# W_down of a decoder layer by seven block products, with tokens as the stationary operand

## The chip, the cores and the metric

One core of a Trainium2 chip runs the whole kernel as one program. The metric is the device time of one execution in microseconds; three runs of the kernel before gave 1706.38, 1706.41 and 1708.55 us, median 1706.41. A profiled execution gives the trace that is read here. Its span runs from the first to the last instruction.

TensorE multiplies: a stationary operand of up to 128 x 128 is loaded into its array, and a moving operand of up to 512 columns streams through it into PSUM. VectorE (DVE), ScalarE (ACT) and GpSimd (POOL) do elementwise work; SyncE (SP) issues most transfers. Each engine has its own queue and works through it in order.

## The reference

One layer, 288 tokens (256 of a prompt, 8 x 4 samples), width 2048. The part that matters here is the feed-forward half:

```python
x = layer_norm(ALPHA * x + merged @ w_o, ln1_g, ln1_b)
hid = jnp.square(jax.nn.relu(x @ w_up))              # 2048 -> 8192
x = layer_norm(ALPHA * x + hid @ w_down, ln2_g, ln2_b)   # 8192 -> 2048
```

Before it stand the input projection, a short convolution, a gated delta rule with its states, two output projections, a gated merge and `w_o`. They are the same in both kernels. All inputs and outputs are float32.

## The kernel before, in words

**Three matmuls for one.** A float32 product is made of fp32r matmuls. Each weight block of 512 KB (4 x 128 rows by 256 columns, `raw`) is split: ScalarE casts it to `hi` (`split_hi`, line 179), VectorE subtracts, `lo = raw - hi` (`split_lo`, line 140 in the helper `tt`). The activations have their own high and low parts. The weights stand in the array, 128 x 128 at a time, and the 288 tokens stream: high by high, high by low, low by high (lines 206 to 208).

**Order.** `blocks` is one long list of weight blocks. The main loop takes block `i`: it splits block `i+3`, runs what is due at `i` (evacuations, side work), issues the 24 matmuls of block `i`, and loads block `i+7`. `raw`, `hi` and `lo` have four buffers each. The load on SP's queue waits until VectorE has read the old `raw`.

**Feed-forward.** The 8192 hidden features are taken in four stages of 2048. In a stage, `w_up` makes 8 groups of 256 features (`up_evac`, line 501: norm of the input, ReLU, square, high and low parts `hh`, `hl`), then `w_down` makes 8 groups of 256 output features, summed feature-major in `acc` by VectorE (`down_evac`, line 528). The residual was written there before, during the first up stage (`residual1`, line 477).

**End.** In the last W_down stage each finished group is transposed to token-major (`turned`, line 601) and its statistics are taken. The last two groups are 128 features wide. `final` (line 642) joins the statistics, makes the last norm with small matmuls of rank 3, which carry mean and scale per row, and sends out. Its constants are loaded by `tail_consts` (line 561) and `tail_tiles` (line 575); `tail_rows` (line 592) splits the rows of gain and bias.

Of the kernel before, what the change touches and what calls it, by code (L numbers as in the profile page):

```python
# [16 lines left out]
P = 128  # L17
# [5 lines left out]
KT = D // P  # L23
H = 8
# [16 lines left out]
def _constants():  # L41
# [33 lines left out]
    f["rowlo"] = np.isin(k, (1, 4)) * 1.0  # L75
    early = ("hm", "bo8", "lcum", "lrem", "lcums", "lrems", "lsp", "bm3", "hmask")
    late = ("quart", "rowhi", "rowlo")
# [26 lines left out]
def hybrid_kernel(ctx: ExitStack, tc: tile.TileContext, A):  # L104
# [9 lines left out]
    ap_ = pool("ap")  # L114
    acp = pool("acp", 2, space=PSUM)
# [43 lines left out]
    fill = []  # L159

    def at(i, f):
        due.setdefault(i, []).append(f)


    def load(i):
        if i >= len(blocks):
            return
        gi, r0, k0, _, _ = blocks[i]
        t = wp.tile([P, KB, GW], F32, tag="raw", name=nm("raw"))
# [3 lines left out]
        raw[i] = t  # L173

    def split_hi(i, step=KB):
        if i < len(blocks):
            his[i] = wp.tile([P, KB, GW], F32R, tag="hi", name=nm("hi"))
            for k in range(0, KB, step):
                act.copy(his[i][:, k:k + step], raw[i][:, k:k + step])  # L179

    def split_lo(i, step=KB):
        if i < len(blocks):
            los[i] = wp.tile([P, KB, GW], F32R, tag="lo", name=nm("lo"))
            r = raw.pop(i)
            for k in range(0, KB, step):
                tt(los[i][:, k:k + step], r[:, k:k + step], his[i][:, k:k + step], SUB)

    def matmuls(i):
        gi, r0, k0, first, last = blocks[i]
        if first:  # L190
            gi["ps"] = acp.tile([P, 2, 512], F32, tag="acc", name=nm("acc"))
# [26 lines left out]
    ci = cp.tile([P, CI.shape[1]], I32, name="ci")  # L218
# [19 lines left out]
    hw = cp.tile([P, 24, 28], F32, name="hw")  # L238
    hwa = cp.tile([P, 8, 19], F32, name="hwa")
    lnp = cp.tile([P, 33], F32, name="lnp")  # L240
    wbar = ao0[:, NL - NE:NL - NE + 16 * KT].rearrange("p (k c) -> p k c", c=16)
    arow = cp.tile([P, 2, 8], F32, name="arow")
    epsc = cp.tile([P, 3], F32, name="epsc")
    hmr, bo8 = (cp.tile([P, P], F32R, name=n) for n in ("hmr", "bo8"))
    stB = cp.tile([P, 24, 27], F32, name="stB")
    stA = cp.tile([P, 8, 18], F32, name="stA")
# [130 lines left out]
    def yb_evac(p):  # L377
        def f(ps):
# [4 lines left out]
            t = ph["pool"].tile([P, 2, NT], F32, tag="yt", name=nm("yt"), bufs=2)  # L383
# [13 lines left out]
    def wo_evac(p):  # L397
        q = slice(2 * p, 2 * p + 2)

        def resid(ps):  # L400
            pl = ph["pool"]
            if p == 0:
# [4 lines left out]
                ph["ln"] = [t[:, 5 + u] for u in range(4)]  # L407
# [4 lines left out]
            ph["s"] = pl.tile([P, 2, NT], F32, tag="yt", name=nm("s"), bufs=2)  # L412
# [49 lines left out]
    def norms(ps):  # L462
# [4 lines left out]
        dm, va, av, nb = ph["ln"]  # L467
# [7 lines left out]
        ph["acc"] = ph["pool"].tile([P, KT, NT], F32, tag="R1", name="acc")  # L475

    def residual1(p):
        tl = {}

        def f():  # L480
            _, _, av, nb = ph["ln"]
            q = slice(2 * p, 2 * p + 2)
            t = ph["pool"].tile([P, 2, NT], F32, tag="yt", name=nm("x1"), bufs=2)
# [7 lines left out]
        def f2():  # L491
            for u in range(2):
                k = 2 * p + u
                act.activation(ph["acc"][:, k, :], tl["t"][:, u, :], AF.Identity, bias=lnp[:, 16 + k:17 + k],
                               scale=ALPHA)
        return f, f2
# [4 lines left out]
    def up_evac(c, p):  # L501
        tl = {}

        def f(ps):
            pl = ph["pool"]
            _, _, av, nb = ph["ln"]
            if p == 0:
                ph["hh"] = xp.tile([P, KT, NT], F32R, tag="XH", name=nm("hh"))
                ph["hl"] = xp.tile([P, KT, NT], F32R, tag="XL", name=nm("hl"))
            s = slice(2 * p, 2 * p + 2)  # L510
            r = pl.tile([P, 2, NT], F32, tag="sg", name=nm("r"), bufs=2)
            q = pl.tile([P, 2, NT], F32, tag="yt", name=nm("r2"), bufs=2)
            w = pl.tile([P, 2, 2], F32, tag="w2", name=nm("w2"), bufs=2)
            act.copy(w, ps[:, :, NT:NX])
            tt(q, ps[:, :, 0:NT], bmid(av, 2), MUL)
            for u in range(2):
                stt(q[:, u, :], nb, w[:, u, 0:1], q[:, u, :], MUL, ADD)
                act.activation(r[:, u, :], q[:, u, :], AF.Relu, bias=w[:, u, 1:2])
            tt(q, r, r, MUL)
            tl["q"] = q  # L520

        def f2(ps):
            s = slice(2 * p, 2 * p + 2)
            act.copy(ph["hh"][:, s, :], tl["q"])
            tt(ph["hl"][:, s, :], tl["q"], ph["hh"][:, s, :], SUB)
        return [f, f2]

    def down_evac(c, p):
        def f(ps):
            a = ph["acc"][:, 2 * p:2 * p + 2, :]  # L530
            tt(a, a, ps[:, :, 0:NT], ADD)
        if c == 3:
            if p == 0:
                return [f, lambda ps: None, lambda ps: out_tiles(p)]
            hold = []

            def rest(ps):
                for g in hold:
                    for _ in g:
                        pass  # L540
                if p < 5:
                    tail_rows(p - 1)
            return [f, lambda ps: None, lambda ps: hold.extend(filter(None, [out_tiles(p)])), rest]
        return [f]

    def next_to_last(ps):
        a = ph["acc"][:, 14, :]
        tt(a, a, ps[:, 0, 0:NT], ADD)

    def collect(ps):  # L550
        turned(14)
        fin, bn = ph["fin"], ph["bn"]
        for b in range(2):
            dve.bn_aggr(out=fin[:, b, 1:3], in_=bn[:, b, 0:15])
        dve.tensor_scalar(out=fin[:, :, 2], in0=fin[:, :, 2], scalar1=15.0 * P, scalar2=None, op0=MUL)

        R = ph["R"] = ph["pool"].tile([P, 2, 2, 6], F32R, tag="mv", name="R")
        act.copy(R[:, 1, :, 3:5], bc(ones[:, 0:2], 2))
        act.mul(R[:, 1, :, 5], ones[:, 0:2], 0.0)

    def tail_consts():
        g3 = ph["pool"].tile([P, KT, NT], F32, tag="R2", name="g3").rearrange("p k t -> p (k t)")
        ph["g2"] = g3[:, 0:D]
        ph["gs"], ph["bs"], ph["b0"] = (g3[:, D + 512 * u:D + 512 * u + 512] for u in range(3))
        ph["late"] = g3[:, D + 1536:D + 1536 + CF.shape[1] - NL]
        gps.dma_start(ph["g2"][:, 1024:D], A["ln2_g"][:, 1024:D].to_broadcast([P, D - 1024]))
        gps.dma_start(ph["b0"], A["ln2_b"][:, 1024:1536].to_broadcast([P, 512]))
        gps.dma_start(ph["late"], A["cf"][:, NL:])
        for j in range(4):
            for t, n in (("gs", "ln2_g"), ("bs", "ln2_b")):  # L570
                row = A[n].rearrange("o (k j f) -> o k j f", j=4, f=P)[:, :, j, :]
                gps.dma_start(ph[t][32 * j:32 * j + 32, :].rearrange("p (k f) -> p k f", k=4),
                              row.to_broadcast([32, 4, P]))

    def tail_tiles():
        pl = ph["pool"]
        g4 = pl.tile([P, D + 512], F32R, tag="R4", name="g4")
        ph["m5"], ph["st5"] = g4[0:6, 0:D], g4[0:6, D:D + 512]
        r5 = pl.tile([P, KT * NX], F32, tag="R3", name="r5")
        ph["r5"] = r5[:, 0:2 * D].rearrange("p (a c) -> p a c", a=2)  # L580
# [874 lines left out]
```

## Time and profile before

| what | value |
|---|---|
| median of three runs | 1706.41 us |
| span of the profiled execution | 1703.4 us |
| TensorE busy | 1688.5 us, 99% of the span |
| VectorE, ScalarE, GpSimd busy | 1007.2, 734.1, 133.8 us |
| `lo` on VectorE, 128 x 1024 | 492 times, mean 1239 ns |
| `hi` on ScalarE, 128 x 1024 | 492 times, mean 1046 ns |
| W_down matmuls | 3 x 1024, 288 columns each, from 968.5 to 1687.9 us in four stages |
| mean granted TensorE clock | 0.998 |

How to read the rows: a matmul's duration overlaps its neighbours', so the spacing of starts is its price, not its mean. In a row of a group stand line, engine, operation, output and inputs, shapes and count, then total busy time and mean of one in ns, then the engine's idle time ahead of them with what ended it. In a timeline row stand start, duration, engine, line and operation; "x2" joins two neighbours. In a row of stages stand the window, its length, and busy time with the number of instructions for PE, PEld (weight load), DVE, ACT and POOL, then the granted clock, the transfers' share and GB/s. In the chain of waits the second number of a row is the time that the piece held the end.

### The profile page before, as it was taken

Reading aid. Unit: us, or ns where it says so; the run is one execution under the profiler, and the core shown is the slowest. Engines: PE = TensorE matmul, PEld = TensorE weight load, DVE = VectorE, ACT = ScalarE, POOL = GpSimd, SP = SyncE. Lnnn points to the kernel's source line nnn. Section 1 sums busy time; section 2 is a strip of 40 time slices with the busy share of each in tenths; the row PEclk is TensorE's granted clock in tenths of the full one; section 3 lists DMA queues with packets and bytes.
Section 4 is the critical chain, followed back from the end, with each engine's and each line's share of the span. In section 5 each row is a group of like instructions: output and inputs, shape, how many; then the busy total and the mean of one; then the engine's idle time right before and its main releaser. Section 6 shows DMA issues by size and latency. Waiting matters only on the chain.

```text
span 1703.4 us, 31106 instructions
## 1 busy us (share of the span) xinstructions
PE 1688.5 (99%) x13063; PEld 1668.7 (98%) x13063; DVE 1007.2 (59%) x1296; ACT 734.1 (43%) x1067; POOL 133.8 (8%) x223
## 2 busy tenths in 40 slices
PE   9999999999999999999999999999999999999997
PEld 7999999999999999999999999999999999999997
DVE  5577876758544444456778844566445654466565
ACT  4675626333543333334445533444334433344442
POOL 2232412023300000000010000000000000000000
PEclk9999999999999999999999999999999999999999
DMA  8464456435555555555565555555555555555552
GB/s 244 140 194 139 123 175 200 150 115 180 162 170 169 166 162 170 163 164 165 158 190 174 165 170 161 164 170 162 167 168 161 163 171 162 164 167 164 162 162 80
DMA packets 275097, 279.18 MB, mean 164 GB/s; under 512 B 13131, under 2 KB 270092, under 8 KB 274952
## 3 DMA queue, kind: packets, MB, share of 16 engines
q1 hardware_dynamic: 270414, 265.95, 51.3%
q0 software_dynamic: 4256, 11.12, 2.3%
q8 instruction: 102, 1.67, 0.4%
q14 instruction: 37, 0.30, 0.1%
q10 hardware_dynamic: 288, 0.13, 0.0%
HBM read 269.68 MB, written 7.48 MB: 163 GB/s over the span
## 4 chain that ended last, share of the span: by engine, by line
PE 98%; DVE 1%; DMA 0%; POOL 0%; issue 0%; SPq 0%; ACT 0%; POOLq 0%; ACTq 0%
PE acc L206 31%; PE acc L208 31%; PE acc L207 31%; PE g L1084 1%; DMA xr<-in_x_prompt_dram 0%; PE g L1072 0%; PE g L1231 0%; PE g L1251 0%; PE g L831 0%; DVE w L143 0%; PE g L1254 0%; PE g L1203 0%; PE g L1243 0%; PE g L608 0%; PE g L798 0%; PE g L958 0%
## 5 line engine op out<-in xcount | busy, mean ns | idle before, releaser
L140 DVE TENSOR_TENSOR lo<-raw,hi 128x1024 fp32r<-128x1024 f32 (+2 forms) x502 | 614.0, 1226 | 556.2 <-ACT hi L179 553.7
L179 ACT CAST hi<-raw 128x1024 fp32r<-128x1024 f32 (+1 forms) x498 | 517.6, 1041 | 765.0 <-PE acc L207 707.7
L206 PE MATMUL acc<-xh,hi 128*128 128x288 f32 x1408 | 422.9, 300 | 0.0
L208 PE MATMUL acc<-xh,lo 128*128 128x288 f32 x1408 | 416.7, 296 | 0.0
L207 PE MATMUL acc<-xl,hi 128*128 128x288 f32 x1408 | 416.5, 296 | 0.0
L206 PE MATMUL acc<-dh,hi 128*128 128x290 f32 x1024 | 303.9, 297 | 0.0
L207 PE MATMUL acc<-dl,hi 128*128 128x290 f32 x1024 | 303.3, 296 | 0.0
L208 PE MATMUL acc<-dh,lo 128*128 128x290 f32 x1024 | 302.7, 296 | 0.0
L206 PE MATMUL acc<-hh,hi 128*128 128x288 f32 x1024 | 302.3, 295 | 0.0
L208 PE MATMUL acc<-hh,lo 128*128 128x288 f32 x1024 | 302.3, 295 | 0.0
L207 PE MATMUL acc<-hl,hi 128*128 128x288 f32 x1024 | 302.3, 295 | 0.0
L206 PEld LDWEIGHTS acc<-xh,hi 128*128 128x128 f32 x1408 | 265.4, 189 | 2.6 <-issue 0.7
L207 PEld LDWEIGHTS acc<-xl,hi 128*128 128x128 f32 x1408 | 265.8, 189 | 0.5
L208 PEld LDWEIGHTS acc<-xh,lo 128*128 128x128 f32 x1408 | 265.6, 189 | 0.0
L206 PEld LDWEIGHTS acc<-dh,hi 128*128 128x128 f32 x1024 | 193.6, 189 | 0.1
L208 PEld LDWEIGHTS acc<-dh,lo 128*128 128x128 f32 x1024 | 193.3, 189 | 0.0
L207 PEld LDWEIGHTS acc<-dl,hi 128*128 128x128 f32 x1024 | 193.3, 189 | 0.1
L207 PEld LDWEIGHTS acc<-hl,hi 128*128 128x128 f32 x1024 | 192.5, 188 | 0.0
L208 PEld LDWEIGHTS acc<-hh,lo 128*128 128x128 f32 x1024 | 192.3, 188 | 0.0
L206 PEld LDWEIGHTS acc<-hh,hi 128*128 128x128 f32 x1024 | 192.1, 188 | 0.0
L207 PE MATMUL acc<-ml,hi 128*128 128x288 f32 x256 | 75.6, 295 | 0.0
L208 PE MATMUL acc<-mh,lo 128*128 128x288 f32 x256 | 75.6, 295 | 0.0
(404 smaller groups left out, 1620.0 us busy)
## 6 DMA issues: line engine op xcount, KB each, us to landing
raw<-in_w_in_dram SPq DMA_DIRECT2D x176, 512.0 KB, 3.5
raw<-in_w_up_dram SPq DMA_DIRECT2D x128, 512.0 KB, 3.9
raw<-in_w_down_dram SPq DMA_DIRECT2D x128, 512.0 KB, 3.7
raw<-in_w_o_dram SPq DMA_DIRECT2D x32, 512.0 KB, 3.7
raw<-in_w_a_out_dram SPq DMA_DIRECT2D x16, 512.0 KB, 3.7
raw<-in_w_b_out_dram SPq DMA_DIRECT2D x16, 512.0 KB, 3.6
S<-in_state_gdn_dram POOLq DMA_DIRECT2D x8, 512.0 KB, 7.8
out_dram<-S POOLq DMA_DIRECT2D x8, 512.0 KB, 4.9
```

Of the source, the lines that this page charges most:

```text
L140: dve.tensor_tensor(out=out, in0=a, in1=b, op=op)
L179: act.copy(his[i][:, k:k + step], raw[i][:, k:k + step])
L206: pe.matmul(o, wh, xh_, start=st, stop=False)
L207: pe.matmul(o, wh, xl_, start=False, stop=False)
L208: pe.matmul(o, wl, xh_, start=False, stop=en)
L1084: pe.matmul(out[r, q * 64:q * 64 + 64], a[r, q, :], b[r, q, :], start=True, stop=True)
```

## The change

For W_down the operands change places: 128 tokens stand in the array, 512 weight columns stream. Two token blocks, two slabs of 128 hidden features and two halves of 1024 output columns make 2 x 2 by 2 x 2 blocks, whose product is formed by seven block products in place of eight.

- A **pair** is two slabs by 1024 columns, loaded as two `raw` tiles of 512 KB (`n1`, `n2`: the column halves). It is three entries of the list: A, B, C. `pair_hi` makes the sums of weights on GpSimd: two of 512 columns in A (`v13`), two in B (`v24`), and casts to `hi` on ScalarE; `pair_lo` makes `lo` on VectorE. In A there is a fourth product's weight, 512 columns more (`h22`, `l22`). `v13` and `v24` have one buffer each.
- Each pair has 7 x 3 fp32r matmuls of 512 columns. A group (8 pairs) holds all eight PSUM banks: seven products and the samples.
- The 32 sample tokens don't take part: four float32 matmuls a pair, 32 x 128 stationary, each with 512 columns of the raw weights into its own quarter of a bank. They come for two pairs at once.
- `up_evac` forms the seven factors of the tokens: squares into `F[0:4]`, three differences on GpSimd, one on VectorE; then high and low parts of 896 columns.
- The sum is token-major (`Y`). `residual1` transposes the residual in the first up stage, one step every three blocks, and puts the samples' part into `xs`. After a group VectorE adds the products from PSUM, GpSimd three SBUF terms.
- In the last stage GpSimd issues the transfers for the norm's constants, and four of the eight 512-column blocks get their statistics and gain early. The norm's end is written anew.
- Raw loads keep four buffers and get two more in the feed-forward half; they are issued when a buffer is free (`advance`). Small tensors move from `cp` to a pool that closes at the merge.

The core of the diff:

```diff
+    def pair_hi(i, kind):
+        a = i - "ABC".index(kind)
+        (n1, _), (n2, _) = raw[a]
+        pl = ph["pool"]
+        h = wide_(his[i])
+        if kind == "A":
+            v = ph["v13"]
+            gps.tensor_tensor(out=v[:, 0], in0=n1[:, 0], in1=n2[:, 0], op=ADD)
+            gps.tensor_tensor(out=v[:, 1], in0=n2[:, 1], in1=n2[:, 0], op=ADD)
+            act.copy(h, n1)
+            his[i, 3] = pl.tile([P, 512], F32R, tag="h22", name=nm("h22"), bufs=2)
+            act.copy(his[i, 3], n2[:, 1])
+        elif kind == "B":
+            v, v4 = ph["v13"], pl.tile([P, 2, 512], F32, tag="yt", name=nm("v24"))
+            ph["v24"] = v4
+            gps.tensor_tensor(out=v4[:, 0], in0=v[:, 0], in1=n2[:, 1], op=ADD)
+            gps.tensor_tensor(out=v4[:, 1], in0=v4[:, 0], in1=n1[:, 1], op=ADD)
+            act.copy(h, v)
+        else:
+            act.copy(h, ph["v24"])
+
+    def pair_lo(i, kind):
...
+        if kind == "A":
+            tt(l, n1, h, SUB)
+            los[i, 3] = ph["pool"].tile([P, 512], F32R, tag="l22", name=nm("l22"), bufs=2)
+            tt(los[i, 3], n2[:, 1], his[i, 3], SUB)
+        elif kind == "B":
+            tt(l, ph["v13"], h, SUB)
+        else:
+            tt(l, ph["v24"], h, SUB)
+            done_with(a)
...
+    def samples(a):
+        gi, _, k0, first, last = blocks[a]
+        n1, n2 = (t for t, _ in raw[a])
+        ps = gi["g"]["ps"]["s"]
+        for q in range(4):
+            u, h = q % 2, q // 2
+            pe.matmul(ps[32 * q:32 * q + 32, :], ph["hs"][:, k0 + u, :], (n1, n2)[h][:, u, :], start=first, stop=last)
+        done_with(a)
...
+    def product(gi, j, f, h, l, first, last):
+        o = gi["ps"][f]
+        fh, fl = ph["fh"][j][:, f - 1, :], ph["fl"][j][:, f - 1, :]
+        pe.matmul(o, fh, h, start=first, stop=False)
+        pe.matmul(o, fl, h, start=False, stop=False)
+        pe.matmul(o, fh, l, start=False, stop=last)
...
+            fv = F[:, 0:4].rearrange("p (u b) t -> p u (b t)", u=2)
+            tt(fv, r[:, :, 0:NP_], r[:, :, 0:NP_], MUL)
+            def sub(o, a, b):
+                gps.tensor_tensor(out=F[:, o], in0=F[:, a], in1=F[:, b], op=SUB)
+            sub(4, 0, 2)
+            sub(5, 1, 0)
+            sub(6, 4, 1)
+            stt(F[:, 7], F[:, 6], -1.0, F[:, 3], MUL, SUB)
...
+            if part == 0:
...
+                act.copy(tl["t"], ps[1])
+                tt(Y(1, 0), Y(1, 0), ps[1], ADD)
+                tt(Y(1, 0), Y(1, 0), ps[3], ADD)
+                tt(Y(1, 1), Y(1, 1), ps[7], SUB)
+            elif part == 1:
+                tt(Y(1, 1), Y(1, 1), ps[4], ADD)
+                tt(Y(2, 1), Y(2, 1), ps[4], ADD)
+            else:
+                t, u = tl["t"], tl["u"]
+                tt(t, t, ps[6], ADD)
+                tt(u, t, ps[5], ADD)
+                tt(Y(2, 0), Y(2, 0), ps[2], ADD)
+                gps.tensor_tensor(out=Y(1, 1), in0=Y(1, 1), in1=t, op=SUB)
+                gps.tensor_tensor(out=Y(2, 0), in0=Y(2, 0), in1=u, op=ADD)
+                gps.tensor_tensor(out=Y(2, 1), in0=Y(2, 1), in1=u, op=SUB)
...
+        for j in range(NPAIR):
+            for kind in "ABC":
+                gi = dict(kind=kind, g=G, W=A["w_down"][0], col0=1024 * g)
+                blocks.append((gi, 2048 * c + 256 * j, 2 * j, j == 0, j == NPAIR - 1))
...
+    def early(b, n):
+        def f():
+            y = block_(b, n)
+            dve.bn_stats(out=ph["bn"][:, b, n, :], in_=y)
+            gps.tensor_tensor(out=y, in0=y, in1=ph["g2"][:, 512 * n:512 * n + 512], op=MUL)
+        return f
...
+    def final():
...
+        tt(Y(1, 0), Y(1, 0), ps[1], ADD)
+        tt(Y(1, 1), Y(1, 1), ps[4], ADD)
+        tt(Y(2, 1), Y(2, 1), ps[4], ADD)
+        tt(Y(2, 1), Y(2, 1), ps[5], SUB)
+        tt(Y(2, 0), Y(2, 0), ps[5], ADD)
+        tt(t, t, ps[6], ADD)
+        tt(Y(2, 1), Y(2, 1), t, SUB)
+        gps.tensor_tensor(out=Y(1, 1), in0=Y(1, 1), in1=t, op=SUB)
+        tt(Y(2, 0), Y(2, 0), t, ADD)
+        dve.bn_stats(out=bn[:, 0, 3, :], in_=block_(0, 3))
+        tt(Y(2, 0), Y(2, 0), ps[2], ADD)
+        dve.bn_stats(out=bn[:, 0, 2, :], in_=block_(0, 2))
...
+        sample_end()
+        tt(Y(1, 1), Y(1, 1), ps[7], SUB)
+        dve.bn_stats(out=bn[:, 1, 3, :], in_=block_(1, 3))
+        tt(Y(1, 0), Y(1, 0), ps[3], ADD)
+        dve.bn_stats(out=bn[:, 1, 2, :], in_=block_(1, 2))
+        wide_of(0)
+        row(0)
+        row(1)
+        wide_of(1)
+        for b in range(2):
+            for n in (2, 3):
+                scale(b, n, gps if n == 2 else dve)
+        ends(0)
+        ends(1)
...
-                at(mark["up"] + 6 + 4 * p + n, f)
+                at(mark["up"] + 6 + 3 * p + n, f)
...
         matmuls(i)
-        load(i + AHEAD + 4)
+        advance()
```

More of the change, by code (lines that the diff above doesn't have):

```diff
@@ L172, in load @@
                      gi["W"][r0:r0 + kb * P, gi["col0"]:gi["col0"] + cols].rearrange("(k p) c -> p k c", p=P))
[L173 to L186 removed]
+        raw[i] = t, s_
@@ new lines, in advance, with room2 @@
+    def advance():
+        while ahead[0] < len(blocks):
+            i = ahead[0]
+            kind = blocks[i][0].get("kind")
+            n = nraw[0] if i >= mark["up"] else None
+            if kind == "A":
+                if not (room(n) and room(n + 1)) or home(n) == home(n + 1) and not room2(n):
+                    return
+            elif not kind and not room(n):
+                return
+            load(i)
+            ahead[0] += 1
+    def room2(n):
+        h = held[home(n)]
+        r = 2 if home(n) == "x" else 4
+        return len(h) < r - 1 or h[1 - r] in free
@@ L1338, in hybrid_kernel @@
     los[0] = wp.tile([P, KB, GW], F32R, tag="lo", name=nm("lo"))
-    t = raw.pop(0)
+    t, s_ = raw.pop(0)
+    free.add(s_)
     for k in range(KB + 2):
```

558 lines of the change are left out of this document (315 added, 243 removed).

## The prediction

> **What bounds the kernel now.** I read the page first (span, shares, chain), then the busy time by stage, then the groups of instructions by shape.
>
> ```profile
> span 1703.4 us, 31106 instructions
> PE 1688.5 (99%) x13063; PEld 1668.7 (98%) x13063; DVE 1007.2 (59%) x1296; ACT 734.1 (43%) x1067; POOL 133.8 (8%) x223
> ...
> PE 98%; DVE 1%; DMA 0%; POOL 0%; issue 0%; SPq 0%; ACT 0%; POOLq 0%; ACTq 0%
> ```
>
> TensorE is never without work, and the chain that ended last is 98% TensorE. VectorE (59%) and GpSimd (8%) look free. The span is 3.0 us under the 1706.41 us median of the runs; I sum against the span and add 3.0.
>
> The stage windows (first up stage; the four W_down stages; the tail), columns PE, PEld, DVE, ACT, POOL, clock:
>
> ```profile
> 864.90:968.54 103.64, 103.64 (x774) 103.43 (x773) 84.91 (x109) 53.47 (x80) 5.99 (x11) 1.00 0.60 179
> 968.54:1070.52 101.98, 101.98 (x771) 101.98 (x770) 49.19 (x48) 35.97 (x38) 0.00 (x0) 1.00 0.53 166
> 1173.18:1275.16 101.98, 101.98 (x771) 101.98 (x770) 46.91 (x44) 35.01 (x36) 0.00 (x0) 1.00 0.53 166
> 1377.82:1479.80 101.98, 101.98 (x771) 101.98 (x770) 46.90 (x44) 34.99 (x36) 0.00 (x0) 1.00 0.53 166
> 1582.46:1688.10 105.64, 105.64 (x803) 105.53 (x801) 61.36 (x100) 37.98 (x50) 0.10 (x1) 1.00 0.43 131
> 1688.10:1703.40 15.30, 6.40 (x35) 3.79 (x34) 7.18 (x28) 5.53 (x12) 2.53 (x2) 0.77 0.43 154
> ```
>
> W_down is 3 x 101.98 + 105.64 = 411.6 us, all matmul: 768 of 288 columns a stage, 101.98/768 = 133 ns each. GpSimd does nothing there.
>
> **TensorE's new price.** A 512-column fp32r matmul stands in the timeline at 220 us, two in a row, and float32 passes stand in the chain:
>
> ```profile
> 220.32 0.63 PE L1203 MATMUL g<-vm,kr 128*128 128x512 f32 x2
> 220.79 0.29 PE L206 MATMUL acc<-xh,hi 128*128 128x288 f32 x1
> ...
> 155.10 1.90 PE g L1072 x32
> 200.04 0.89 PE g L1231 x8
> 877.89 0.97 PE g L466 x4
> ```
>
> Two take 220.79 - 220.32 = 0.47, so 0.235 each. A pair of 128-row slabs on 1024 columns needs 7 products x 3 = 21 of them: 4.93 us, where the old form took 48 x 0.133 = 6.38. The samples come back as float32: a float32 matmul is two passes (L466 has 4 for two matmuls), 0.2425 us for 288 columns, so 0.431 for 512 and 0.862 a matmul. A pair has four, each on its own strip of 32 array columns. If all four run together that is 0.86, one after the other 3.45. Passes on 64-column strips (L1072) take 1.90/32 = 59 ns where whole-array ones of the same 128 columns (L1231) take 111, so two strips do overlap; I take 0.86. TensorE's pair is then 4.93 + 0.86 = 5.79 us (at worst 8.38). Were it still the bound, a stage would be 16 x 5.79 = 92.6 us, 9.4 less than now.
>
> **What the change adds on VectorE and GpSimd.** Per pair, the weights need three hi/lo splits of 1024 elements and one of 512, and four sums of 512 elements, which the diff puts on GpSimd (two for block A, two for B). Rows for one of each:
>
> ```profile
> L140 DVE TENSOR_TENSOR lo<-raw,hi 128x1024 fp32r<-128x1024 f32 x492 | 608.7, 1239 | 552.6 <-ACT hi L179 550.2
> L140 DVE TENSOR_TENSOR lo<-raw,hi 128x512 fp32r<-128x512 f32 x6 | 3.9, 688 | 3.6 <-ACT hi L179 3.5
> L179 ACT CAST hi<-raw 128x1024 fp32r<-128x1024 f32 x492 | 514.2, 1046 | 761.7 <-PE acc L207 707.7 <-issue 41.4 <-ACT hi L179 8.6
> L737 POOL TENSOR_TENSOR r<-r,g 128x512 f32<-128x512 f32 x1 | 1.3, 1260 | 0.1
> L140 DVE TENSOR_TENSOR S<-S,g 128x512 f32<-128x512 f32 x16 | 10.2, 676 | 0.3 <-PE g L1203 0.3
> ```
>
> Alone, VectorE needs 3 x 1.24 + 0.69 = 4.41, GpSimd 4 x 1.26 = 5.04, ScalarE 3 x 1.05 and a half one = 3.7: each under 5.79. But the timeline shows what happens when the two meet:
>
> ```profile
> 177.19 1.04 POOL L1146 TENSOR_TENSOR kr<-kr,rsc 128x512 f32<-128x512 f32 x1
> 177.42 1.90 DVE L140 TENSOR_TENSOR lo<-raw,hi 128x1024 fp32r<-128x1024 f32 x1
> ...
> 205.59 1.22 DVE L140 TENSOR_TENSOR lo<-raw,hi 128x1024 fp32r<-128x1024 f32 x1
> 205.81 2.76 POOL L1192 TENSOR_TENSOR vm<-v,cf 128x1024 fp32r<-128x1024 f32 x1 [8.85 <-PE g L1243]
> ...
> 207.25 2.40 DVE L140 TENSOR_TENSOR lo<-raw,hi 128x1024 fp32r<-128x1024 f32 x1
> ...
> 217.24 1.28 DVE L140 TENSOR_TENSOR S<-S,g 128x512 f32<-128x512 f32 x2
> 217.44 1.90 POOL L1192 TENSOR_TENSOR vm<-v,cf 128x1024 fp32r<-128x1024 f32 x1 [5.17 <-PE g L1203]
> 218.44 1.98 DVE L140 TENSOR_TENSOR lo<-raw,hi 128x1024 fp32r<-128x1024 f32 x1
> ```
>
> Each `lo` that starts under a GpSimd operation ends 1.08 to 1.09 us after that one's end: 179.32 against 178.23, 209.65 against 208.57, 220.42 against 219.34. It did not run beside it, it stood. The other way round: `vm` at 205.81 met a `lo` that ended at 206.81, and ended 1.76 after that; unhindered (217.44) it took 1.90. So a two-input GpSimd operation and a VectorE subtraction with both inputs in SBUF take turns. An add with one input in PSUM (S<-S,g, 0.64 each under `vm`) does not stand.
>
> So the pair's bound is a sum: 3 x 1.08 + (0.69 - 0.14) = 3.79 for VectorE, and 4 x 1.19 = 4.76 for GpSimd (1.26 alone, 1.12 after a turn, since 0.14 of the start is hidden; the middle). **8.55 us a pair, against TensorE's 5.79.** TensorE then waits for `lo` in every block, and its saving and the samples' price (up to 8.38) are both hidden.
>
> [...]
>
> **The sum.** A stage has 2 groups of 8 pairs: 16 x 8.55 = 136.8. Each group's evacuation adds three GpSimd operations of 512: 6 x 1.19 = 7.1. Its eight PSUM adds (0.68 each, 10.9 for both groups) don't take turns, but on VectorE the next subtractions are queued behind them, and TensorE's next group waits for the banks they free (it fills all eight); I count them whole (bounds 0 to 10.9). The first pair is prepared under the last up blocks: -8.5. A stage is 146.3, four are 585.2: **+173.6** against 411.6.
>
> Smaller terms. Last stage: four GpSimd products for the norm, 4.8, and 18 transfers issued by GpSimd:
>
> ```profile
> L572 POOL DMA_DIRECT2D g<-in_ln_g_dram x4 | 2.2, 552 | 1.3 <-DMA g<-in_ln_b_dram 1.3
> L608 PE MATMUL g<-cf,acc 128*128 128x128 f32 x32 | 5.0, 274 | 0.5 <-DVE acc L140 0.5
> ...
> raw<-in_w_down_dram SPq DMA_DIRECT2D x128, 512.0 KB, 3.7
> ...
> 1694.54 2.18 DVE L143 SCALAR_TENSOR_TENSOR Y<-Y,r,g 128x512 f32<-128x512 f32 x3
> ```
>
> 18 x 0.55 = 9.9, of which VectorE can use about half: +5 (0 to 9.9). The 32 transposes move from the last W_down stage into the first up stage, where TensorE is still the bound: 32 x 0.11 (L1231's spacing; their busy time is 5.0) = +3.5. There VectorE is at 84.91 of 103.64; the three differences on GpSimd, for which VectorE waits, and the longer `fl` (896 elements) add, estimated from the `lo` rows by length, 1.8 us to each of 8 groups, 99.3 in all, and the residual comes every 3 blocks instead of 4: +2 (0 to 6). Other up stages have room. The raw loads keep their number and 512 KB; they land in 3.7 us and a pair lasts 8.5, so they cost nothing. Tail: after the last subtraction VectorE has eleven adds and four statistics of 512 (15 x 0.68 = 10.2) while TensorE has 12 matmuls left (2.8). Then come the two token blocks' norm values, one after the other (some nine short operations each, estimated 3.5 in all), the scaling in two turns (2 x 1.26 = 2.5), four outputs (2.18/3 each, 2.9), and what followed the last output before (1703.4 - 1696.7 = 6.7): 25.8 - 2.8 = 23.0 against 15.3: +8 (5 to 15).
>
> 1703.4 + 173.6 + 4.8 + 5 + 3.5 + 2 + 8 = 1900.3, and 3.0 around the span: **1903 us**. All terms low (GpSimd 1.04, no evacuation): pair 7.95, stage 124.9, total 1807. All high (9.45, stage 161.3): 1980. Own range 1807 to 1980.
>
> **Rivals.**
> - *They don't stand* (faster). Place: the sums of GpSimd beside `lo`. If the plain additions here blocked VectorE under (5.79 - 3.79)/4 = 0.5 us each, TensorE would stay the bound: 4 x 92.6 - 411.6 = -41, +8 tail, +5.5 up: **1679**. For it: only two plain GpSimd operations of 512 are in the trace, without a `lo` beside them. Against: all three `lo` above, and `vm` the other way.
> - *Strips one after the other.* No turns, but four float32 strips in a row: pair 8.38, stage 134.1, +125 and 13.5: **1845**. Against: L1072's 59 ns.
> - *The clock falls as well.* TensorE would work 5.79 of 8.55 us (68%). In the tail it worked 6.40 of 15.30 and the mean granted clock was 0.77. At the spacing of the first 20 us, 0.24 instead of 0.133, its pair is 10.4, stage 167, total about **1985**.
>
> ```profile
> 15.63 0.44 PE L207 MATMUL acc<-xl,hi 128*128 128x288 f32 x1
> 15.87 0.44 PE L208 MATMUL acc<-xh,lo 128*128 128x288 f32 x1
> ```
>
> [...]
>
> **Chances.** Forecast 0.81; they don't stand 0.08; strips in a row 0.05; clock 0.04; something between, with no change, 0.02. A difference under 0.2% can't be told from none. Faster 0.08, same 0.02, slower 0.90. The range 1805 to 1985 leaves out the first rival, the last and the edges of the forecast.
>
> **What would show it.** Right: W_down stages of about 146 us each with TensorE busy near two thirds, `lo` with a mean near 2 us, GpSimd sums well above 1.26, TensorE's waits on DVE `lo`. Wrong: `lo` at 1.24 beside GpSimd; matmuls of 512 columns far from 0.235; strips of L1072's kind 0.86 apart; a granted clock under 1. The forecast falls if W_down is under 100 us a stage.

## The result

The changed kernel takes 1969.28 us (median of four runs, 1966.72 to 1971.45) against 1706.65 us for the kernel before: a ratio of 1.1536, with a 95% interval of 1.152 to 1.1552. It is slower, as forecast, and 66 us slower than the 1903 us that were forecast, inside the range of 1805 to 1985.

The page of the kernel after opens with its span and shares; its section 4 gives the shares of the chain of waits.

```profile
span 1968.4 us, 29882 instructions
PE 1768.7 (90%) x11876; PEld 1551.9 (79%) x11876; DVE 1327.9 (67%) x1462; ACT 852.9 (43%) x1251; POOL 700.4 (36%) x609
...
PE 61%; POOL 13%; DVE 12%; issue 9%; ACT 3%; DMA 1%; DVEq 0%; SPq 0%; POOLq 0%; ACTq 0%
```

TensorE has 1187 fewer matmuls (11876 for 13063), and it no longer carries the chain alone: GpSimd and VectorE hold a quarter of it. GpSimd went from 133.8 to 700.4 us.

The windows by stage of the kernel after: first up stage, then W_down and up in turn, the last W_down, the tail. The columns are those of the window rows of before (PE, PEld, DVE, ACT, POOL, clock, transfers, GB/s).

```profile
865.40:992.63 127.23, 117.03 (x822) 112.99 (x821) 93.68 (x120) 66.24 (x115) 15.43 (x25) 0.95 0.41 126
992.63:1143.82 151.19, 112.52 (x453) 67.58 (x449) 125.55 (x88) 60.77 (x73) 122.27 (x67) 0.88 0.38 122
1143.82:1250.18 106.36, 106.36 (x784) 104.76 (x784) 65.60 (x74) 47.70 (x68) 18.49 (x28) 0.98 0.46 144
1250.18:1401.36 151.18, 114.88 (x452) 68.48 (x449) 126.75 (x90) 59.85 (x71) 122.20 (x67) 0.88 0.37 122
1401.36:1508.60 107.24, 107.24 (x785) 105.64 (x785) 65.70 (x74) 47.74 (x68) 18.48 (x28) 0.97 0.46 143
1508.60:1659.86 151.26, 109.19 (x452) 65.41 (x449) 126.85 (x90) 59.83 (x71) 122.31 (x67) 0.93 0.37 122
1659.86:1765.97 106.11, 106.11 (x785) 104.51 (x785) 65.61 (x74) 47.72 (x68) 18.50 (x28) 0.98 0.47 144
1765.97:1939.74 173.77, 126.07 (x494) 75.64 (x490) 113.63 (x105) 58.42 (x73) 130.79 (x88) 0.82 0.27 89
1939.74:1968.40 28.66, 10.92 (x24) 4.94 (x22) 17.44 (x36) 5.72 (x13) 6.74 (x5) 0.62 0.23 82
```

Set against the windows of before, the 265.0 us by which the span grew divide up so (the first matmul of the first up stage comes 0.5 later):

| part | before | after | grew by | forecast | missed by |
|---|---|---|---|---|---|
| first up stage | 103.64 | 127.23 | 23.6 | 5.5 | 18.1 |
| three W_down stages | 3 x 101.98 | 151.19, 151.18, 151.26 | 147.7 | 133.0 | 14.7 |
| last W_down stage | 105.64 | 173.77 | 68.1 | 50.4 | 17.7 |
| three later up stages | 3 x 102.66 | 106.36, 107.24, 106.11 | 11.7 | 0 | 11.7 |
| tail | 15.30 | 28.66 | 13.4 | 8 | 5.4 |

(Before, the second to fourth up stage lasted 102.66 us each, from the end of one W_down stage in the prediction's windows to the start of the next.) Four fifths of the growth is W_down.

**Inside a W_down stage.** The groups of instructions of the second W_down stage, GpSimd's sums first (busy time, mean of one in ns, idle time ahead):

```profile
L271 POOL TENSOR_TENSOR ffn<-raw 128x512 f32<-128x512 f32 x10 | 21.8, 2178 | 0.0
L279 POOL TENSOR_TENSOR v<-v,raw 128x512 f32<-128x512 f32 x10 | 18.7, 1866 | 0.8
L278 POOL TENSOR_TENSOR v<-ffn,raw 128x512 f32<-128x512 f32 x10 | 18.5, 1853 | 0.0
L270 POOL TENSOR_TENSOR ffn<-raw,raw 128x512 f32<-128x512 f32 x10 | 17.9, 1789 | 8.0 <-DVE lo L144 8.0
```

```profile
L144 DVE TENSOR_TENSOR lo<-ffn,hi 128x1024 fp32r<-128x1024 f32 x16 | 29.7, 1857 | 3.4 <-ACT hi L280 3.4
L144 DVE TENSOR_TENSOR lo<-raw,hi 128x1024 fp32r<-128x1024 f32 x12 | 24.4, 2037 | 0.0
L144 DVE TENSOR_TENSOR lo<-v,hi 128x1024 fp32r<-128x1024 f32 x16 | 21.1, 1317 | 18.8 <-ACT hi L282 18.6
L144 DVE TENSOR_TENSOR l<-raw,h 128x512 fp32r<-128x512 f32 x10 | 16.6, 1656 | 0.0
```

A sum that takes 1.26 us alone lasts 1.79 to 2.18, a `lo` of 1.24 lasts up to 2.04, an `l` of 0.69 lasts 1.66. Only `lo<-v` is nearly its own length: it is the last of its pair, after both sums of block B.

The timelines of GpSimd and of VectorE in one pair of that stage (start, duration):

```profile
1290.20 2.33 POOL L270 TENSOR_TENSOR ffn<-rawx,rawx 128x512 f32<-128x512 f32 x1 [1.17 <-DVE lo L144]
1292.49 2.28 POOL L271 TENSOR_TENSOR ffn<-rawx 128x512 f32<-128x512 f32 x1
...
1298.65 1.26 POOL L270 TENSOR_TENSOR ffn<-raw,raw 128x512 f32<-128x512 f32 x1
```

```profile
1290.16 1.23 DVE L144 TENSOR_TENSOR lo<-v,hi 128x1024 fp32r<-128x1024 f32 x1
1291.30 2.32 DVE L144 TENSOR_TENSOR lo<-rawx,hi 128x1024 fp32r<-128x1024 f32 x1
1293.54 1.78 DVE L144 TENSOR_TENSOR l<-rawx,h 128x512 fp32r<-128x512 f32 x1
```

The `lo` of 1290.16 ends at 1291.39; the sum that began under it ends 1.14 later, at 1292.53; the `lo` of 1291.30 ends 1.09 after that, at 1293.62; the sum of 1292.49 ends 1.15 after that, at 1294.77; `l` ends 0.55 later. Each waits for the other's end. From one L270 to the next is 8.45 us here, and 8.51 on the average of the six pairs from 1273.18 to 1324.21: the pair, forecast at 8.55.

What TensorE waits for in that stage (total, times, longest), the two largest rows:

```profile
PE acc L320 <- DVE lo L144: 9.4, 16, 1.4
PE acc L318 <- ACT hi L282: 7.1, 7, 1.0
```

The first is the wait for `lo` that was forecast. The second was not: it is the wait for ScalarE's cast of block C's sum, which in turn stands for GpSimd (217.2 us over the whole kernel).

The samples' matmuls of two pairs in TensorE's timeline:

```profile
1061.64 1.93 PE L310 MATMUL g<-raw,ffn 128*32 128x512 f32 x16
```

Sixteen passes in 1.93 us: the four strips do run together. In the trace four passes start within 0.02 us (1061.64 to 1061.67), and the fours follow each other at 0.43 to 0.45 us.

**The clock.** In the trace of the kernel after, the granted clock is 1.00 or 0.50, and from 840 to 1940 us its changes lie whole multiples of 3.41 us apart. Windows of 3.41 us, TensorE's busy time in the second column, the granted clock in the third from last:

```profile
1263.55:1266.96 3.41, 1.12 (x4) 0.30 (x2) 3.25 (x3) 2.51 (x3) 3.41 (x3) 1.00 0.63 225
1266.96:1270.38 3.42, 3.34 (x12) 1.54 (x16) 3.42 (x3) 1.04 (x1) 3.37 (x2) 0.52 0.00 0
1280.62:1284.03 3.41, 1.91 (x6) 0.93 (x6) 1.25 (x2) 2.33 (x3) 3.41 (x3) 1.00 0.33 87
1284.03:1287.44 3.41, 3.38 (x12) 1.49 (x16) 3.41 (x2) 1.23 (x2) 3.33 (x3) 0.52 0.62 225
...
1649.27:1652.68 3.41, 1.93 (x6) 0.97 (x6) 3.16 (x3) 3.41 (x5) 0.00 (x0) 1.00 0.91 292
```

After the first and the third of these windows the clock is halved for one window (0.52 and not 0.50, since these windows begin 0.14 us before the clock's change). This is new: before, the stages were at 1.00.

### The profile page after: what moved, and what is told of

Read it like the earlier page. It is cut to its first block, busy times and chain, and to the rows that moved or that the text cites. A ratio compares the mean times of both kernels' runs of the same rounds, so it can differ in the third digit from the quotient of the medians.

```text
span 1968.4 us, 29882 instructions
## 1 busy us (share of the span) xinstructions
PE 1768.7 (90%) x11876; PEld 1551.9 (79%) x11876; DVE 1327.9 (67%) x1462; ACT 852.9 (43%) x1251; POOL 700.4 (36%) x609
## 4 chain that ended last, share of the span: by engine, by line
PE 61%; POOL 13%; DVE 12%; issue 9%; ACT 3%; DMA 1%; DVEq 0%; SPq 0%; POOLq 0%; ACTq 0%
PE acc L378 19%; PE acc L379 18%; PE acc L380 18%; DVE lo L144 6%; POOL v L279 3%; POOL v L278 3%; POOL ffn L271 3%; POOL ffn L270 2%; ACT hi L282 2%; DVE Y L144 1%; DVE l L144 1%; POOL ffn L715 1%; PE g L1279 1%; ACT r L709 1%; ACT hi L243 1%
## 5 line engine op out<-in xcount | busy, mean ns | idle before, releaser
L144 DVE TENSOR_TENSOR lo<-raw,hi 128x1024 fp32r<-128x1024 f32 (+2 forms) x375 | 496.9, 1330 | 305.4 <-ACT hi L243 304.8
L243 ACT CAST hi<-raw 128x1024 fp32r<-128x1024 f32 (+1 forms) x328 | 339.4, 1038 | 467.2 <-PE acc L379 424.3
L378 PE MATMUL acc<-dh,hi 128*128 128x290 f32 x1024 | 310.3, 303 | 23.6 <-DVE t L144 23.6
L715 POOL TENSOR_TENSOR ffn<-ffn 128x128 f32<-128x128 f32 x96 | 41.5, 461 | 794.0 <-DVE ffn L144 794.0
L282 ACT CAST hi<-v 128x1024 fp32r<-128x1024 f32 x64 | 67.1, 1048 | 223.3 <-POOL v L279 217.2
L144 DVE TENSOR_TENSOR lo<-v,hi 128x1024 fp32r<-128x1024 f32 x64 | 83.4, 1303 | 98.0 <-ACT hi L282 97.3
L144 DVE TENSOR_TENSOR lo<-ffn,hi 128x1024 fp32r<-128x1024 f32 x64 | 112.9, 1764 | 22.6 <-ACT hi L280 22.6
L280 ACT CAST hi<-ffn 128x1024 fp32r<-128x1024 f32 x64 | 67.0, 1047 | 117.1 <-POOL ffn L271 111.3
L318 PE MATMUL acc<-hi,fh 128*128 128x512 f32 x160 | 72.9, 455 | 47.1 <-ACT hi L282 17.1
L144 DVE TENSOR_TENSOR lo<-rawx,hi 128x1024 fp32r<-128x1024 f32 x63 | 96.4, 1532 | 27.0 <-ACT hi L243 27.0
L320 PE MATMUL acc<-lo,fh 128*128 128x512 f32 x160 | 74.7, 467 | 20.3 <-DVE lo L144 20.1
```

Of the source, the lines that this page charges most:

```text
L144: dve.tensor_tensor(out=out, in0=a, in1=b, op=op)
L243: act.copy(his[i][:, k:k + step], raw[i][0][:, k:k + step])
L280: act.copy(h, v)
L282: act.copy(h, ph["v24"])
L318: pe.matmul(o, fh, h, start=first, stop=False)
L320: pe.matmul(o, fh, l, start=False, stop=last)
```

## The experiments

All times are medians of device time; the kernel before took 1705.99 to 1708.17 us beside them. In brackets stand the ratio to it and the ratio's 95% interval.

**No sums.** The four GpSimd sums are left out, and raw halves are split and multiplied in their place in blocks B and C (`n2` in B, `n1` in C, in `pair_hi` and `pair_lo`); all else stays.

```diff
-            gps.tensor_tensor(out=v[:, 0], in0=n1[:, 0], in1=n2[:, 0], op=ADD)
...
-            act.copy(h, v)
+            act.copy(h, n2)
...
-            act.copy(h, ph["v24"])
+            act.copy(h, n1)
```

> The four sums of weights per pair are left out: B and C split and multiply the raw halves, so y_prompt is not the reference's. All else stays (casts, subtractions, matmuls, samples, evacuation). Theory T (GpSimd's sums and VectorE's subtractions take turns at SBUF, 8.5 us a pair): with no sums TensorE is the bound again at 16 x 5.79 = 93 us; the first three W_down stages fall from 151.2 to 93 to 100 us, lo is back at about 1.24 us, the granted clock is 0.99 or more, the whole about 1969 - 4 x 54 = 1750 us. Rival S (the float32 samples hold TensorE, 8.38 us a pair): stages stay above 130 us. Rival K (the lower clock is the cause and not a consequence): the clock stays near 0.88 in these stages and they stay above 120 us.

Measured: 1756.08 us (1.029, 1.0261 to 1.032). Window of its second W_down stage, and the group of its `lo` there:

```profile
1202.13:1303.75 101.62, 92.66 (x453) 65.23 (x449) 81.93 (x88) 60.03 (x68) 7.87 (x7) 0.99 0.56 182
```

```profile
L144 DVE TENSOR_TENSOR lo<-raw,hi 128x1024 fp32r<-128x1024 f32 x32 | 40.0, 1254 | 13.6 <-ACT hi L274 8.3 <-ACT hi L269 2.2 <-ACT hi L276 1.7
```

The sums cost 213 us, and without them `lo` is back at 1254 ns. TensorE's work in a stage is 92.66 us, as the prediction worked out (92.6). But the stage still lasts 101.62, hardly less than before and a little above the 93 to 100 expected: the other 9.0 us are TensorE's waits at the ends of the two groups, 2.7 and 6.3, for the evacuation of the eight banks.

**Fills in place of sums.** GpSimd writes the same tiles twice each with constants; the sums are left out, the order of the work and its buffers stay.

```diff
-            gps.tensor_tensor(out=v[:, 0], in0=n1[:, 0], in1=n2[:, 0], op=ADD)
-            gps.tensor_tensor(out=v[:, 1], in0=n2[:, 1], in1=n2[:, 0], op=ADD)
+            gps.memset(v, 1.0)
+            gps.memset(v, 0.5)
...
+            gps.memset(v4, 1.0)
+            gps.memset(v4, 0.5)
```

> In place of the four sums of 512 columns GpSimd fills the same two buffers with constants, four fills of 1024 columns a pair, so all waits and single buffers stay and GpSimd works about 4 x 1.0 us a pair, but it reads nothing from SBUF; y_prompt is not the reference's. T says that it is the two inputs that are read on both sides: stages of 93 to 105 us, lo near 1.24 us. Rival C (the chain through GpSimd, ScalarE and VectorE with one buffer each for v13 and v24 sets the pace, not the turns): stages stay at 140 to 151 us.

Measured: 1774.18 us (1.0396, 1.0366 to 1.0427), a W_down stage 103.8 us. Groups in its second W_down stage:

```profile
L144 DVE TENSOR_TENSOR lo<-raw,hi 128x1024 fp32r<-128x1024 f32 x12 | 14.7, 1223 | 1.9 <-ACT hi L272 1.1 <-ACT hi L243 0.7
...
L278 POOL MEMSET v<- 128x1024 f32 x15 | 14.3, 956 | 1.0 <-DVE lo L144 1.0
```

GpSimd is still busy 3.82 us of each pair (four fills of 956 ns), in the same chain and with one buffer each, and `lo` does not stand: it takes 1223 ns. So it is not the chain from sum to cast to `lo`, nor the single buffers: what was taken out is that GpSimd reads SBUF (and each fill is 0.3 us shorter than a sum alone, which is no more than 1.2 us a pair). The same group takes 1223 ns here, beside fills that read nothing, against 2037 under the sums.

**Sums on VectorE.** The whole computation; `gps.tensor_tensor` becomes `dve.tensor_tensor` in the four sums.

> The four sums are made by VectorE in place of GpSimd, nothing else is changed; the result is the whole computation. T: no turns, but VectorE now needs 3 x 1.13 + 0.6 + 4 x 0.6 + 0.68 (evacuation) = 7.1 us a pair, more than TensorE's 5.79, so stages of about 114 us, and 1969 - 4 x 37 = 1820 us in all. C: the chain is as long as before, stages at 140 us or more. If VectorE could hide the sums: 93 to 100 us.

Measured: 1847.42 us (1.0826, 1.0794 to 1.0857), stages of 121.8, 122.8, 122.8. Window of its second W_down stage:

```profile
1220.75:1343.53 122.78, 101.41 (x453) 68.12 (x449) 119.37 (x148) 59.17 (x70) 6.79 (x7) 0.92 0.46 150
```

VectorE works 119.37 of 122.78 us: it alone is the bound now. The 114 us expected had the adds at the group ends in it (0.68 a pair), but nothing for the factors of the last up group, which are made when W_down has begun: there the distance from one L270 to the next is 12.26 us, where a pair takes 6.69, so 5.6 more. The other 3 us were not taken apart.

**Half the sums on VectorE.** Those of block B move, those of A stay on GpSimd; the whole computation.

> The two sums of block B go to VectorE, those of block A stay on GpSimd. Theory (all of the pair's operations with two SBUF inputs on the two engines add up, whoever does them): a pair is 3 x 1.08 + 0.55 + 2 x 0.69 + 2 x 1.19 = 7.55 us, 1.0 less than 8.55; stages 151.2 - 16 = 135 us, about 1905 us in all (1898 to 1912). Rival (not the turns but the chain of four dependent sums, of which block B's are the late ones): stages as with all sums on VectorE, 122 us, 1850 us in all.

Measured: 1899.47 us (1.1132, 1.111 to 1.1154).

```profile
1235.45:1371.92 136.47, 101.65 (x453) 64.77 (x449) 133.15 (x119) 60.16 (x71) 71.61 (x37) 0.95 0.41 135
```

A stage of 136.5 (forecast 135), between 122.8 and 151.2. Each pair of sums that leaves GpSimd takes about 14 us off a stage, or 0.9 us off a pair. The cost adds up by operation, as turns do; the late sums of B are not special.

**Samples twice.** The samples' matmuls are issued twice, so the samples' part is doubled.

```diff
+        for q in range(4):
+            u, h = q % 2, q // 2
+            pe.matmul(ps[32 * q:32 * q + 32, :], ph["hs"][:, k0 + u, :], (n1, n2)[h][:, u, :], start=False, stop=last)
```

> The samples' four float32 matmuls a pair are issued twice (the samples' part is then twice as large), 16 x 0.86 = 13.8 us more of TensorE work in each W_down stage. Theory (VectorE and GpSimd in turns set the pair's 8.5 us, TensorE has 2.7 us of room): stages stay at 151 us, 1963 to 1975 us in all. Rival (part of the pair is TensorE's, at its lower clock): up to 55 us more, 2024 us; a half of it would be 1997 us.

Measured: 1970.85 us (1.155, 1.1527 to 1.1573), against 1969.28.

```profile
1252.84:1402.31 149.47, 119.62 (x564) 70.88 (x561) 125.06 (x88) 58.80 (x68) 121.11 (x67) 0.90 0.37 123
```

Sixteen pairs at 0.86 are 13.8 us more of TensorE work a stage, and the stage is not longer. (Its busy time grew by 4.7 only; the ends of matmuls are modelled, so I read no more from that.) TensorE's time in W_down, with its half clock, is hidden under the turns.

**Residual one block later.** In the first up stage the third step of each transposed piece comes one block later, so that ScalarE is done before TensorE gets there.

```diff
-        for n, f in enumerate(residual1(p)):
+        for n, f in zip((0, 1, 3), residual1(p)):
             at(mark["up"] + 6 + 3 * p + n, f)
```

> In the first up stage the residual's four transposes are issued one block later, so that TensorE does not stand before them while ScalarE is late; everything else as after the change. Theory R (of the 23.6 us that this stage got longer, about 10 are TensorE's wait for ScalarE at the transposes, 7 the lower clock that follows such pauses, 3.5 the transposes): the stage falls from 127.2 to 110 to 115 us, the whole by 12 to 17 us. Rival D (VectorE is overloaded by the residual in these blocks, wherever the transposes stand): the stage stays within 4 us.

The waits of the kernel after in that stage (total, times, longest) show why I tried it:

```profile
PE g L683 <- ACT x L676: 9.9, 8, 3.4
```

Measured: 1957.86 us (1.1473, 1.144 to 1.1506). Its window of the first up stage:

```profile
866.38:979.48 113.10, 110.84 (x822) 107.40 (x820) 91.63 (x119) 63.93 (x114) 15.47 (x25) 1.00 0.45 142
```

14.1 us less in this stage, 11.4 in the whole (just under the 12 to 17 expected), since the next stage took 1.6 more. The clock is 1.00 where it was 0.95, and TensorE's wait for ScalarE at the transposes is 2.3 us where it was 9.9.

**Constants by SyncE.** The 18 transfers are issued by SyncE instead of GpSimd (`gps.dma_start` becomes `sp.dma_start` in `tail_tiles` and `tail_rows`). GpSimd's timeline of the kernel after shows them between two sums:

```profile
1777.26 2.35 POOL L279 TENSOR_TENSOR v<-v,rawx 128x512 f32<-128x512 f32 x1
1779.55 0.58 POOL L783 DMA_DIRECT2D g<-in_ln_g_dram  x1
...
1783.12 0.50 POOL L787 DMA_DIRECT2D g<-in_ln_b_dram  x1
1787.80 0.50 POOL L787 DMA_DIRECT2D g<-in_ln_g_dram  x1 [4.18 <-DMA g<-in_ln_g_dram]
...
1789.06 1.27 POOL L270 TENSOR_TENSOR ffn<-raw,raw 128x512 f32<-128x512 f32 x1
```

> The 18 transfers of the norm's constants are issued by SyncE in place of GpSimd, nothing else changes. Theory (issuing by GpSimd takes time away from the sums and from VectorE, part of the 22.6 us by which the last W_down stage is longer than the others): 5 to 10 us less, 1959 to 1964 us, and the last stage near 165 us. Rival (the last stage is longer because of its statistics and products, and the transfers cost nothing): 1967 to 1971 us. Second rival (SyncE then stands at the waits for the rows' buffer, and the raw loads behind it come late): over 1971 us.

Measured: 1960.63 us (1.149, 1.1472 to 1.1507), 8.7 less.

```profile
1765.90:1930.20 164.30, 120.83 (x495) 74.42 (x492) 122.18 (x105) 58.46 (x73) 124.27 (x70) 0.86 0.29 94
```

The last stage falls by 9.5, from 173.77 to 164.30. Beside the issue time there was, in the kernel after, a wait of 4.18 us of GpSimd for its own earlier transfer to land, with the next pair's first sum behind it.

**The rest without sums.** The sums left out as in the first experiment, and with it the residual one block later, the constants by SyncE, and the four early products on VectorE.

> The four sums of weights are left out (raw halves in their place), the residual's third step comes one block later, the constants' transfers are issued by SyncE, and the four early products of the norm run on VectorE. Theory (what is left is the group ends, the first up stage and the tail): 1756 less 11.4 (the residual, by its own run) less 5 to 10 (transfers): 1735 to 1740 us, still slower than 1706. Rival (the mends don't add up, since the last stage is VectorE's): 1744 us. Rival on the other side (with nothing in turns the last stage reaches 93 us): 1715 us or less.

Measured: 1735.25 us (1.0166, 1.0149 to 1.0183). Even if sums cost nothing, this form with these three mends is 28.5 us behind the kernel before.

**All of it, with sums.** The same with the sums on VectorE; the whole computation.

> The whole computation, with what the other runs point to: the four sums of weights on VectorE, the residual's third step one block later, the constants' transfers issued by SyncE, the four early products of the norm on VectorE. Theory (the steps add up, since each lies in another stage): 1847.4 with the sums on VectorE, less 11.4 for the residual, less 8.7 for the transfers: 1827 us, still slower than 1706. Rival (with the sums on VectorE the last stage is VectorE's alone, and GpSimd's transfers and products did not hold it): 1836 us. Rival on the other side (the last stage loses GpSimd's products too, which still blocked VectorE): 1820 us or less.

Measured: 1833.41 us (1.0741, 1.0723 to 1.0759), the fastest whole computation of this form, between the two expectations. Windows of its last stage and tail:

```profile
1667.90:1802.10 134.20, 105.92 (x494) 69.79 (x491) 126.50 (x167) 57.73 (x72) 5.93 (x6) 0.92 0.35 115
1802.10:1831.10 29.00, 10.84 (x24) 4.82 (x22) 17.32 (x36) 5.72 (x13) 6.73 (x5) 0.60 0.23 82
```

The first up stage gave its 14.1 again, but the last stage and the tail only 2.9 (166.1 with the sums on VectorE alone, 163.2 here). The likely reason, for which no run was made, is that with no sums on GpSimd its transfers hold up little, and that VectorE, busy 126.50 of 134.20, takes on the four products.

**Filling the pause.** Behind each of the first three W_down stages TensorE waits 7.87 us for VectorE's evacuation, and the clock is halved over the start of the up stage (0.50 over its first 3.81, 5.69 and 3.19 us). 26 matmuls that nobody reads go into that pause.

```diff
+            if last and g["stage_end"]:
+                fh = ph["fh"][j]
+                for _ in range(26):
+                    pe.matmul(g["ps"]["s"], fh[:, 1, :], h[:, 1], start=True, stop=True)
```

> After the last product of each of the first three W_down stages, 26 more matmuls of 512 columns go into the samples' bank, which has been read by then; nobody reads what they write. They are 26 x 0.23 = 6.0 us in a pause of 8.3 us. Theory (the clock falls after any stretch of 3.4 us in which TensorE was busy for less than some 1.9, and a half clock of 7 to 10 us at the start is why an up stage takes 106.1 to 107.2 where it took 102.7): the three later up stages take 102.7 to 103.5, the W_down stages stay at 151.2, all in all 10 to 12 us less, 1957 to 1960 us. Rival (the up stages are longer by VectorE's and GpSimd's work on the factors): 1967 to 1972 us.

Measured: 1973.74 us (1.1558, 1.1539 to 1.1578). The expectation failed. ScalarE's timeline shows that the fill itself held what comes next, the buffer of `hi` that it reads:

```profile
1402.42 1.04 ACT L243 CAST hi<-rawx 128x1024 fp32r<-128x1024 f32 x1 [5.12 <-PE g L352]
```

The W_down stages grew to 153.1, and of the clock's half only one window (3.41 us) was left in the up stage, which took 106.2 all the same. The same fill on top of all the other steps:

> The whole computation: the sums of weights on VectorE, the residual one block later, the transfers issued by SyncE, the early products on VectorE (1833.4 us together), and the 26 filling matmuls at the end of the first three W_down stages. Theory (clock at the starts of the up stages): 1833 less 3 x 3.8 = 1822 us (1820 to 1825). Rival (the up stages' excess is not the clock's): 1833 us. Both are over 1707.

Measured: 1839.86 us (1.0778, 1.076 to 1.0796), 6.5 more than without it. The reason is the same: ScalarE waits 16.3 us in all for the fills, in three places.

**Filling with other data.** The moving operand is the low part of the tokens, so that no buffer of weights is held.

```diff
+                fh, x5 = ph["fh"][j], ph["fl"][0][:, 0:4, :].rearrange("p a b -> p (a b)")
+                    pe.matmul(g["ps"]["s"], fh[:, 1, :], x5, start=True, stop=True)
```

> The 26 filling matmuls again, on the kernel after the change, with the low parts of the tokens as their moving operand, so that they do not hold the buffer of the weights' high parts for which ScalarE waited 5.12 us in the first try. Theory (an up stage is 102.7 us, plus 1.72 us of samples' matmuls that fall into it, plus half of its time at the half clock): the three later up stages take 104.4 to 105.0, the W_down stages 151.2; 1969.3 less 5 to 6: 1963 to 1964 us. Rival (their excess is the work on the factors): 106.4, 107.2 and 106.1 as they were, 1969 us.

Measured: 1964.34 us (1.1499, 1.148 to 1.1518). The W_down stages take 151.2 us as before. Window of the up stage behind the second one:

```profile
1401.61:1506.29 104.68, 104.68 (x784) 103.08 (x784) 65.68 (x74) 47.72 (x68) 18.53 (x28) 1.00 0.47 146
```

The three up stages take 104.69, 104.68 and 104.69. So their excess of 3.9 us on average was 1.72 of samples' matmuls that fall into them, under 0.4 of other things, and the rest, 1.9, the half clock that the pause brings. This fill was not run on top of the other steps.

## Why the prediction was right, and where it was short

**Right: the engines take turns, and that is the bound.** The pair is 8.51 us against 8.55 forecast, the hand-overs 1.14 and 1.09 us against 1.12 and 1.08. The fills show that it is the reading (`lo` 1223 ns, 2037 under the sums), half the sums show that the costs add, the doubled samples show that TensorE's work is hidden. The rival *they don't stand* fell by 290 us. Its own place, though, was priced rightly: with no sums TensorE's stage has 92.66 us of work (and 1.72 of its samples' matmuls stand ahead of it, in the up stage). The 9.45 a pair in "All high" (4 x 1.26 + 4.41, each operation at its whole length) is shown by no run; 8.51 was measured.

**Right: the strips.** Two pairs of samples take 1.93 us; in a row they would take 6.9 (16 x 0.431). *Strips one after the other* fell.

**Short by 14.7: three W_down stages, 4.9 each.** What was counted came out. Fifteen pairs (the first is prepared ahead) are 127.7 us at 8.51 each, against 128.3. The two group ends, from the distances between GpSimd's L270, are 18.1 against 18.0 (7.1 + 10.9): 6.0 at the first and 12.1 at the second (from the end of GpSimd's last sum, 1389.91, to the stage's end, with 0.6 at its start). "I count them whole" gave 9.0 to each, so the sum agrees with some luck. The step that failed is "Other up stages have room": the factors were priced in the first up stage alone, but the last up group of every stage makes its factors when W_down has begun, where VectorE and GpSimd are the bound. GpSimd's queue at the start of the second W_down stage:

```profile
1250.81 2.20 POOL L270 TENSOR_TENSOR ffn<-raw,raw 128x512 f32<-128x512 f32 x1 [2.17 <-DVE lo L144]
...
1258.85 1.29 POOL L715 TENSOR_TENSOR ffn<-ffn 128x128 f32<-128x128 f32 x3 [3.63 <-DVE ffn L144]
...
1263.78 2.13 POOL L270 TENSOR_TENSOR ffn<-rawx,rawx 128x512 f32<-128x512 f32 x1
```

The three differences (L715) wait for VectorE's squares, and the sums stand behind them. From L270 to L270 is 12.97 us, and 9.40 to the one after it, against 8.51 elsewhere: 5.4 us a stage, which the sum had at nothing. The first and the third stage show 12.97 and 9.39, 12.95 and 9.41. No run moved the factors, so this is read from the trace alone.

At the second group's end VectorE also does subtractions for the next blocks between the adds. TensorE's last product starts at 1393.11 and its next matmul at 1401.36; in VectorE's timeline between them:

```profile
1396.35 1.22 DVE L144 TENSOR_TENSOR lo<-rawx,hi 128x1024 fp32r<-128x1024 f32 x1
1397.49 1.28 DVE L144 TENSOR_TENSOR Y<-Y,acc 128x512 f32<-128x512 f32 x2
1398.68 1.22 DVE L144 TENSOR_TENSOR lo<-rawx,hi 128x1024 fp32r<-128x1024 f32 x1
```

The run without sums has waits at the group ends too, 9.0 us a stage. They are also why TensorE's saving of 9.4 us a stage would not have been had in any case.

**Short by 18.1: the first up stage.** The step was "the residual comes every 3 blocks instead of 4: +2 (0 to 6)". It was 14.1: I asked whether VectorE had room, and what was late was ScalarE's part of the residual, for which TensorE stood 8 times, 9.9 us, with half the clock behind it (a mean of 0.95 over the stage). When a step is moved, each of its producers has to be followed. Another 1.7 are samples' matmuls that fall into the stage, and the last 2.3 are the waits for ScalarE that the later transposes leave.

**Short by 17.7: the last stage.** 4.9 are those of the other stages. 18 issues at 0.55 were right as a size, 9.9, but "VectorE can use about half" was not: 9.5 is what they cost. Without those transfers the last stage is still 13.1 over the other stages (164.3 against 151.2), where four products at 1.19 were taken (4.8). In the trace of that run the four pairs with an early product take 10.57 to 10.64 us from L270 to L270, 8.4 more than four pairs of 8.51: GpSimd stands before each product for VectorE's statistics, which are queued behind its splits. In the kernel after, this wait is

```profile
POOL Y L812 <- DVE g L811: 8.3, 4, 2.4
```

The four pairs beside which the rows of gain and bias are split take 9.82 to 10.14, 6.0 more in all, for which the sum had no term. The stage's end is 1.5 shorter. No run took the products or the rows out by themselves.

**Short by 11.7: the later up stages,** which I had at nothing ("Other up stages have room"). They had: VectorE and GpSimd did not hold them. The half clock at their starts did (1.9 us a stage on average), and the samples' 1.72. What did not have room was the W_down stage behind them, which takes their last group's factors.

**Short by 5.4: the tail.** Its granted clock is 0.62, against 0.77 before. That this is the cause is argued, not shown.

**The clock rival** was given 0.04 and held in part. The clock does fall, to a mean of 0.88 in two W_down stages (a sign that the prediction listed as one of being wrong), but it decides nothing there, since TensorE's work is hidden; it costs in the stages where TensorE is the bound, 1.9 us a stage on average in the later up stages. The rival's price, all pairs at half speed, did not come about. That the pauses, 2.8 us a pair (8.55 less 5.79) and cut in three, were too short to lower the clock was my own estimate, which no trace had shown, and it failed: the window 1280.62 to 1284.03 has 1.91 us of work, and its longest pause is 1.00, from 1281.80 to 1282.80, and the clock fell (0.52 in the next window).

## What to carry to other kernels

Before elementwise work is given to an idle GpSimd, look for a row where one of its operations meets a VectorE operation with two SBUF inputs: if the one that began second ends about its own length after the other's end (here a `lo` of 1.24 us ended 1.09 after the sum's end), their times are to be added, and an engine at 8% beside one at 59% is no free room. A saving on the engine that bounds a kernel (here 9.4 us of 102 a stage) is worth only what the next engine leaves of it, at the ends of groups too, and with the work of the stage before that falls into it. Where TensorE stops being the bound, count its half clock at the start of the next stage in which it is the bound again (here 1.9 us a stage on average).

## What the runs showed of the hardware that I had not expected

**The clock fell without an idle window.** I went through the kernel after from 840 to 1940 us in windows of 3.41 us along the clock's changes. Each of the 31 drops to half came after a window in which TensorE was busy 1.91 us or less (56%); after every full-clock window with 1.93 us or more it stayed; between 1.5 and 1.91 both occur. In nine of these windows no pause was longer than 1.03 us. At half clock, it came back after windows with 2.85 us or more, but some with up to 3.25 left it at half. The bounds are good to some 0.15 us: laid exactly on the changes, the window of 1.91 has 1.88, and that of 2.85 has 2.99.

**A fill must not hold a buffer.** 26 matmuls in a pause of 7.9 us cost 4.5 us in the whole when they read the last `hi`, and gained 4.9 when they read something else.

**An engine that issued transfers waited for its own:** after eight issues in a row GpSimd stood 4.18 us before the ninth, until the first, issued at 1779.55, had landed at 1787.52. In the trace the ninth issue carries a wait for semaphore 101, which the first transfer signals, so this wait stands in the program; a limit of the queue is not shown.
